# Nineteen small SBUF copies beside the last stores of a ReLU linear-attention kernel

## The chip, the cores and the metric

The kernel runs on one core of one Trainium2 chip. The metric is the device time of one execution in microseconds; the two runs of the kernel before took 126.61 and 126.70 us, with a median of 126.66 us. A profiled execution of the same kernel gives the trace that is read here. Its span, from the first to the last instruction, is 124.8 us.

## The reference

Q, K and V have the shape 8 x 12 x 512 x 64 in fp32, so there are 96 heads of 512 rows of 64 values.

```python
Q_feat = np.maximum(0, Q)
K_feat = np.maximum(0, K)
KV = np.einsum('bhkd,bhkv->bhdv', K_feat, V)
K_sum = np.sum(K_feat, axis=2)
numerator = np.einsum('bhqd,bhdv->bhqv', Q_feat, KV)
denominator = np.einsum('bhqd,bhd->bhq', Q_feat, K_sum)
return (numerator / (denominator[:, :, :, None] + 1e-10)).astype(np.float32)
```

Each input and the output is 12.6 MB in fp32. The trace counts 37.75 MB read from HBM and 12.58 MB written.

## The kernel before

**Tiling.** Eight heads make an octet, and there are twelve octets (`NO = 12`), numbered 0 to 11 in the code; the "tenth octet" is octet 9. K and V are loaded by groups of four heads, two groups to an octet. One octet of the output is one tile `o_sb` of 128 partitions by 2048 fp32, which is 1 MiB.

**Loads.** The first two K and V groups are loaded as fp32 by SP (SyncE) in four transfers at the very start (L115, L116), K and V of a group into the two halves of one tile. All other loads are issued by POOL (GpSimd), which converts fp32 to bf16 on the way: `load_kv` (L101 for a whole octet, L105 for single groups) and `load_q` (L109). They are traced in one loop ahead of all computation, so on POOL they are queued one behind the other: 12 of Q, 14 of K and 14 of V, 40 in all. The pool of K tiles and the pool of V tiles have six buffers each, the pool of Q tiles seven.

**Computation.** For each octet DVE and ACT prepare K and V (`prep`, L144 and L146; `prep_v`, L151 or L153), PE makes K'V (`mm_kv`, L158), ACT copies the result out (L168), PE transposes Q (L179), PE computes the transposed output (L209) and the denominators (L229), PE turns the output back (L247), and DVE multiplies by the reciprocal in `norm` (L253) into `o_sb`, in two halves.

**Stores.** `store(o, o_sb)` is called after the second `norm` of an octet and issues on SP. For octets 0 to 6 it issues first a copy of 128 bytes from the K tile of the octet five ahead into the tile `scratch` (L261): that copy waits for this load, and since SP takes its instructions in order, the store behind it waits too. Then it issues the 1 MiB store (L268). Octets 7 to 9 have only the store. The last octet is stored in two halves (L266), each behind its half of `norm`; octet 10 has one store. Nothing ever reads `scratch`. Over the whole program SP issues 24 transfers: 4 loads, 7 scratch copies, 11 whole stores and 2 half stores.

**Order.** The schedule is by hand (`tc.manual_schedule()`): each engine takes its instructions in the order in which the program names them, and the framework adds the semaphore waits. A DMA signals its landing by a semaphore. At the end of the program (L371) SP waits for every transfer that is still out.

Of the kernel before, what the change touches and what calls it, by code (L numbers as in the profile page):

```python
# [10 lines left out]
def kernel(  # L11
# [7 lines left out]
    nc = tc.nc  # L19
# [12 lines left out]
    NO = NG // 2  # L32
# [5 lines left out]
    fp32 = mybir.dt.float32  # L38
# [4 lines left out]
    def pool(name, bufs, **kw):  # L43
        return ctx.enter_context(tc.tile_pool(name=name, bufs=bufs, **kw))

    consts = pool("consts", 1)
# [18 lines left out]
    ident32 = consts.tile([P, P], fp32, name="ident32")  # L65
# [13 lines left out]
    mask = consts.tile([P, 2, 2], fp32, name="mask")  # L79
    scratch = consts.tile([1, D], bf16, name="scratch")  # L80

    mask_h = consts.tile([P, 8, 2], fp32, name="mask_h")

    qt_sb = [consts.tile([P, U, P], bf16, name=f"qt{i}") for i in range(NZ)]
# [174 lines left out]
    def store(o, o_sb):  # L259
        if o + DELAY < NO:  # L260
            nc.sync.dma_start(out=scratch, in_=k_sb[2 * (o + DELAY)][0:1, 0, :])  # L261
        Ov = Or[o].rearrange("p (r d) -> p r d", d=D)
        if o == NO - 1:
            for j in range(2):
                rs = slice(RQ // 2 * j, RQ // 2 * (j + 1))
                nc.sync.dma_start(out=Ov[:, rs], in_=o_sb[:, rs])  # L266
            return
        nc.sync.dma_start(out=Ov, in_=o_sb)  # L268

    def out_tile():  # L270
        return outp.tile([P, RQ, D], fp32, name="o_sb", tag="o_sb")
# [19 lines left out]
    def backs(o):  # L291
        o_sb = out_tile()
        for j in range(2):
            norm(o, j, back(o, j), o_sb)
        store(o, o_sb)
# [26 lines left out]
    o = NO - 2  # L322
# [15 lines left out]
    for i in range(2):  # L338
        relu_q(o + 1, i, transp(o + 1, i), nc.vector if i == 1 else None)
    norm(o, 1, ps, o_sb)  # L340
    store(o, o_sb)
    idle(5, o + 1)
    out_u(o + 1, 0)
# [32 lines left out]
```

## Time and profile before

| What | us |
|---|---|
| median of two runs | 126.66 |
| span of the profiled execution | 124.8 |
| PE busy | 84.2 |
| DVE busy | 81.2 |
| ACT busy | 78.8 |
| POOL busy | 26.1 |
| last `norm` (L253) starts / lasts | 117.1 / 1.2 |
| last half store issued / time to landing | 118.3 / 5.6 |

The times are those of one execution, counted from the first instruction. "SPq" is the queue of SP: its DMA instructions are listed with the time that the issue took, not the time of the transfer. "To landing" is the time from the start of the issue to the signal that the transfer is complete. Waits for the landing of a transfer stand as separate EVENT_SEMAPHORE instructions where the DMA instruction has another wait of its own. The DMA share is the mean busy share of the 16 DMA engines; records overlap a little, so it can exceed 1.

### The profile page before, as it was taken

How to read it: one execution, taken by the hardware profiler on the slowest of the kernel's cores; microseconds unless marked ns; L12 is line 12 of the kernel's file. 1: busy time of each engine (PE TensorE's matmuls, PEld its weight loads, DVE VectorE, ACT ScalarE, POOL GpSimd, SP SyncE). 2: the span in 40 equal slices, each digit the busy share in tenths (PEclk: the TensorE clock that was granted, in tenths of full speed). 3: DMA queues.
4: the chain of work that ended last, by engine and by line, in shares of the span. 5: the costliest groups of instructions: out<-in, count | busy, mean ns of one | idle time of the engine just before them, and what ended most of it. 6: DMA issues, size and time to landing. Idle time of an engine off the chain costs nothing.

```text
span 124.8 us, 2646 instructions
## 1 busy us (share of the span) xinstructions
PE 84.2 (67%) x1075; PEld 76.8 (62%) x1075; DVE 81.2 (65%) x176; ACT 78.8 (63%) x114; POOL 26.1 (21%) x46
## 2 busy tenths in 40 slices
PE   0041096988989898982994790999597397798400
PEld 0040095977978786871993790799495395788300
DVE  2615852979797988729727925965909909978700
ACT  0250639999898979955944973667759556747000
POOL 6922133222332223011121111124031000000000
PEclk9999999999999999999589998559999999999995
DMA  3999999999999999999999999999999999999993
GB/s 116 332 282 275 218 207 211 213 212 215 207 214 213 210 219 283 293 223 262 317 216 246 339 212 211 356 229 231 343 223 217 337 246 216 316 421 423 428 412 129
DMA packets 10492, 32.67 MB, mean 262 GB/s; under 512 B 1136, under 2 KB 1136, under 8 KB 9072
## 3 DMA queue, kind: packets, MB, share of 16 engines
q0 software_dynamic: 7808, 17.83, 74.5%
q1 hardware_dynamic: 2672, 14.68, 29.3%
q8 instruction: 8, 0.13, 0.4%
q14 instruction: 4, 0.03, 0.1%
HBM read 37.75 MB, written 12.58 MB: 403 GB/s over the span
## 4 chain that ended last, share of the span: by engine, by line
DVE 32%; DMA 30%; PE 22%; ACT 6%; issue 2%; SPq 1%; DVEq 1%; ACTq 0%
DMA v_sb<-in_V_dram 22%; DVE o_sb L253 15%; PE ps_kv L158 11%; DMA kv_first<-in_V_dram 8%; PE ps_bk L247 6%; DVE kf L144 5%; ACT kvd L168 3%; DVE vo L146 3%; PE ps_qt L179 3%; DVE vo L153 2%; DVE den L237 2%; DVE rec L241 2%; DVE own L232 2%; ACT qt L187 2%; ACT vo L151 1%
## 5 line engine op out<-in xcount | busy, mean ns | idle before, releaser
L158 PE MATMUL ps_kv<-vo,kf 128*128 128x132 bf16 x384 | 30.1, 240 | 18.9 <-ACT vo L151 8.0
L158 PEld LDWEIGHTS <-kf 128*128 128x128 bf16 x384 | 27.3, 107 | 20.5 <-DVE vo L146 10.8
L253 DVE TENSOR_TENSOR o_sb<-ps_bk,rec 128x1024 f32<-128x1024 f32 x24 | 28.3, 1219 | 11.3 <-PE ps_bk L247 11.3
L168 ACT CAST kvd<-ps_kv 64x260 bf16<-64x260 f32 (+1 forms) x54 | 18.7, 346 | 16.4 <-PE ps_kv L158 14.3
L211 ACT COPY ot_sb<-ps_ot 128x1024 f32<-128x1024 f32 x22 | 21.9, 1015 | 5.4 <-PE ps_ot L209 4.8
L247 PE MATMUL ps_bk<-ident,ot_sb 128*128 128x128 f32 x192 | 23.0, 273 | 0.0
L144 DVE TENSOR_SCALAR kf<-k_sb,mask 128x1024 bf16<-128x1024 bf16 x44 | 18.3, 458 | 6.6 <-DMA k_sb<-in_K_dram 6.6
L187 ACT ACTIVATE qt<-ps_qt 128x1024 bf16<-128x1024 bf16 x23 | 22.4, 1029 | 0.1
L247 PEld LDWEIGHTS ps_bk<-ident,ot_sb 128*128 128x128 f32 x192 | 20.8, 141 | 0.0
L209 PE MATMUL ps_ot<-qt,kvd 128*128 128x256 bf16 x88 | 13.5, 283 | 10.4 <-DVE o_sb L253 10.2
L209 PEld LDWEIGHTS <-kvd 128*128 128x128 bf16 x88 | 8.4, 100 | 13.1 <-issue 12.1
L179 PE MATMUL ps_qt<-ident,q_sb 128*128 128x128 bf16 x192 | 14.8, 238 | 0.0
L146 DVE TENSOR_SCALAR vo<-v_sb,mask 128x1024 bf16<-128x1024 bf16 x22 | 10.7, 484 | 5.6 <-DMA v_sb<-in_V_dram 5.6
L151 ACT ACTIVATE vo<-v_sb,mask 128x1024 bf16<-128x1024 bf16 x10 | 11.5, 1154 | 4.0 <-DMA v_sb<-in_V_dram 3.8
L179 PEld LDWEIGHTS <-q_sb 128*128 128x128 bf16 x192 | 13.5, 108 | 0.5 <-DMA q_sb<-in_Q_dram 0.2
L109 POOL DMA_DIRECT2D q_sb<-in_Q_dram x12 | 7.3, 612 | 20.4 <-DMA k_sb<-in_K_dram 10.2
L229 PEld LDWEIGHTS <-qt 128*128 128x128 bf16 x192 | 6.7, 96 | 4.8 <-ACT qt L187 3.4
L229 PE MATMUL ps_den<-kvd,qt 128*128 128x16 bf16 x192 | 7.5, 179 | 2.7 <-ACT qt L187 2.2
L101 POOL DMA_DIRECT2D v_sb<-in_V_dram x8 | 5.7, 718 | 11.5 <-DMA q_sb<-in_Q_dram 7.6
L101 POOL DMA_DIRECT2D k_sb<-in_K_dram x8 | 5.6, 704 | 9.3 <-DMA v_sb<-in_V_dram 5.5
L232 DVE SCALAR_TENSOR_TENSOR own<-ps_den,mask_h 128x256 f32<-128x256 f32 x12 | 5.0, 417 | 3.3 <-PE ps_den L229 3.3
L105 POOL DMA_DIRECT2D k_sb<-in_K_dram x6 | 3.4, 568 | 15.9 <-DMA k_sb<-in_K_dram 8.0
(29 smaller groups left out, 39.0 us busy)
## 6 DMA issues: line engine op xcount, KB each, us to landing
out_dram<-o_sb SPq DMA_DIRECT2D x11, 1024.0 KB, 8.8
q_sb<-in_Q_dram POOLq DMA_DIRECT2D x12, 512.0 KB, 20.1
k_sb<-in_K_dram POOLq DMA_DIRECT2D x8, 512.0 KB, 21.3
v_sb<-in_V_dram POOLq DMA_DIRECT2D x8, 512.0 KB, 21.1
k_sb<-in_K_dram POOLq DMA_DIRECT2D x6, 256.0 KB, 17.7
v_sb<-in_V_dram POOLq DMA_DIRECT2D x6, 256.0 KB, 17.0
kv_first<-in_K_dram SPq DMA_DIRECT2D x2, 512.0 KB, 5.7
kv_first<-in_V_dram SPq DMA_DIRECT2D x2, 512.0 KB, 7.2
```

What stands on the lines that cost most here:

```text
L144: nc.vector.tensor_scalar(kf[g][:, :, s, :], k_sb[g], scalar1=0.0, scalar2=mask[:, 0, s:s + 1], op0=Alu.max, op1=Alu.mult)
L146: nc.vector.tensor_scalar(vo[g % NB][:, :, 0, 2:D + 2], v_sb[g], scalar1=mask[:, 1, 0:1], scalar2=None, op0=Alu.mult)
L151: nc.scalar.activation(vo[g % NB][:, :, 1, 2:D + 2], v_sb[g], Act.Copy, scale=mask[:, 1, 1:2])
L158: nc.tensor.matmul(ps_kv[:, g % 2, 0:2 * (D + 2)].rearrange("p (t d) -> p t d", t=2), kf[g][:, r, :, :].rearrange("p s d -> p (s d)"), vo[ ...
L168: copy(kvd[o % NK][64 * c:64 * c + 64, 4 * gs.start + s:4 * gs.stop:2, c * D1:c * D1 + D1].rearrange("p (g t) d -> p g t d", t=2), ps_kv[6 ...
L179: nc.tensor.transpose(ps[:, u, :], q_sb[o][:, i * (U // 2) + u, :], ident)
L187: nc.scalar.activation(to, ps, Act.Relu)
L209: nc.tensor.matmul(ps[:, i], kvd[o % NK][:, h, 1:2 * D + 1], q[:, :, h, :], start=True, stop=True, skip_group_check=True)
L211: nc.scalar.copy(ot[o][:, :, 4 * j:4 * j + 4], ps.rearrange("p h u c -> p u h c"))
L229: nc.tensor.matmul(ps[:, u], qt_sb[o % NZ][:, u, :], kvd[o % NK][:, :, 0:2 * D1:2 * D1 - 1], start=True, stop=True, skip_group_check=True)
L247: nc.tensor.transpose(ps[:, 2 * v:2 * v + 2].rearrange("p c d -> p (c d)"), ot[o][:, 8 * j + v].rearrange("p h c -> p (h c)"), ident32)
L253: nc.vector.tensor_tensor(o_sb[:, rs], ps, rec[o][:, rs].unsqueeze(2).to_broadcast([P, 16, D]), op=Alu.mult)
```

## The change

A tile `marks` is added (16 partitions by 24 x 80 fp32, 7680 bytes in each partition). Behind the store of octet 9, SP issues fifteen copies from the identity matrix `ident32` (fp32, in SBUF) into rows of `marks`: the first has 15 partitions, the last has 1, and each has its own row size, 32 + 2k fp32 for k partitions (248 bytes for k = 15, 136 for k = 1). Each goes to a free-dimension range of `marks` that no other copy writes. Four more, of 3, 5, 2 and 1 partitions with rows of 64 + 2k fp32, are issued by GpSimd; in the program they come at the same place, but since GpSimd has only the loads in its queue ahead of them, they stand directly behind its last load. Nobody reads `marks`; the output and its computation are as before.

```diff
@@ -79,6 +79,7 @@
     scratch = consts.tile([1, D], bf16, name="scratch")
 
+    marks = consts.tile([16, 24, 80], fp32, name="marks")
     mask_h = consts.tile([P, 8, 2], fp32, name="mask_h")
@@ -266,6 +267,11 @@
             return
         nc.sync.dma_start(out=Ov, in_=o_sb)
+        if o == NO - 3:
+            for k in range(15, 0, -1):
+                nc.sync.dma_start(out=marks[0:k, k, 0:32 + 2 * k], in_=ident32[0:k, 0:32 + 2 * k])
+            for k in (3, 5, 2, 1):
+                nc.gpsimd.dma_start(out=marks[0:k, 16 + k, 0:64 + 2 * k], in_=ident32[0:k, 0:64 + 2 * k])
 
     def out_tile():
```

## The prediction

> **What bounds the kernel now.** I read the engine table first (PE 67%, DVE 65%, ACT 63%: no engine is full), then the chain of waits, then the stages of the tail, then SP's queue. The chain ends with the last `norm`; what follows it is only the store of its result. The table of stages shows what the tail is (us, then busy us and instruction counts of PE, PEld, DVE, ACT and POOL, then granted clock, DMA share, GB/s):
>
> ```profile
> 105.00:110.00 5.00, 4.14 (x52) 3.83 (x49) 4.93 (x13) 2.98 (x6) 0.00 (x0) 1.00 1.07 316
> 110.00:115.00 5.00, 4.47 (x72) 3.91 (x70) 4.14 (x8) 3.14 (x5) 0.00 (x0) 1.00 1.01 421
> 115.00:120.00 5.00, 1.79 (x17) 1.56 (x15) 2.36 (x2) 0.44 (x1) 0.00 (x0) 1.00 1.00 419
> 120.00:124.80 4.80, 0.00 (x0) 0.00 (x0) 0.00 (x0) 0.00 (x0) 0.00 (x0) 0.64 0.57 230
> ```
>
> The DMA engines are full from 105 us to 121 us: the stores of octets 6 to 11 drain one behind the other. At 419 GB/s a store of 1.049 MB takes 2.5 us. SP's queue (start, issue time) shows why they come together:
>
> ```profile
> 102.78 0.50 SPq L261 DMA_DIRECT2D scratch<-k_sb  x1
> 103.37 10.70 SPq L268 DMA_DIRECT2D out_dram<-o_sb  x5
> 117.21 1.46 SPq L266 DMA_DIRECT2D out_dram<-o_sb  x2
> ```
>
> The scratch copy of octet 6 held the queue until 102.8; four stores (octets 6 to 9) then go out within 2.2 us. The tenth octet's store, and the one after it, one by one:
>
> ```profile
> 105.19 0.33 SPq L268 DMA_DIRECT2D out_dram<-o_sb  x1
> ...
> 113.74 0.33 SPq L268 DMA_DIRECT2D out_dram<-o_sb  x1
> ```
>
> Between them SP stands idle for 8.2 us, and that is where the fifteen copies go. The first of the two lands late:
>
> ```profile
> L268 SPq DMA_DIRECT2D out_dram<-o_sb x1: 333/333/333, 105.2 to 105.2; - x1
> L268 SPq EVENT_SEMAPHORE  x1: 17/17/17, 105.6 to 105.6; - x1
> ...
> DMA to landing us min/median/max: 13.9/13.9/13.9
> ```
>
> 13.9 us after 105.2 is 119.1 us: that is when octet 9's store is complete. The EVENT_SEMAPHORE at 105.6 belongs to the next store (octet 10): a second wait beside that for `norm`. It is the key of this prediction. What it waits for is seen best on POOL at the start:
>
> ```profile
> 1.24 0.65 POOL L109 DMA_DIRECT2D q_sb<-in_Q_dram  x1 [0.79 <-POOLq L360]
> ...
> 6.47 0.71 POOL L101 DMA_DIRECT2D k_sb<-in_K_dram  x1
> 9.43 0.72 POOL L101 DMA_DIRECT2D v_sb<-in_V_dram  x1 [2.25 <-DMA q_sb<-in_Q_dram]
> 13.41 0.56 POOL L109 DMA_DIRECT2D q_sb<-in_Q_dram  x1 [3.27 <-DMA k_sb<-in_K_dram]
> ```
>
> The load at 9.43 is POOL's ninth, and only the third of V, whose pool has six buffers; so it waits for no buffer, yet it waits for the landing of POOL's first load (Q). The tenth waits for the second (K). An engine thus has eight landing semaphores in rotation, and its ninth transfer waits until the first has landed. SP does the same:
>
> ```profile
> L268 SPq EVENT_SEMAPHORE  x7: 17/17/17, 64.3 to 105.6; - x7
> L266 SPq EVENT_SEMAPHORE  x1: 17/17/17, 117.6 to 117.6; - x1
> ```
>
> On whole stores the extra wait begins at 64.3, the third octet's store, SP's tenth transfer. It is missing just where the transfer eight places earlier is a scratch copy that SP had already waited for (octets 7 and 9, first half of octet 11). Today all these waits are for transfers long landed (17 ns each): octet 10's store waits for octet 4's.
>
> **The change, part by part.** Call the copies c1 to c15. In SP's order there now stand: store 6, 7, 8, 9, c1 ... c15, store 10, store 11 in halves. Counting eight back:
> - c1 to c4 wait for store 4, scratch 5, store 5 and scratch 6, issued by 102.8; scratch 6 needs 4.8 us and lands at 107.6. They go out between 105.6 and 108, in SP's idle time: nothing.
> - c5, c6 and c7 wait for stores 6, 7 and 8. These landed 8.1, 10.2 and 12.2 us after 103.37, 103.95 and 104.47, so at 111.5, 114.2 and 116.7. From here SP is held, store 10 (ready at 113.7) behind it.
> - c8 waits for store 9: 119.1 us. The copies queued behind that store cannot shift its landing.
> - c9 to c15 wait for c1 to c7, which sit in the queue behind store 9 and carry 19 KB together. I take it that they land within a few tenths of 119.1, so these waits cost nothing; only the issues count.
>
> So from 119.1 on, SP has to issue eight copies, c8 to c15, before store 10. The trace has no copy of this shape. The nearest row is the scratch copy, also small and SBUF to SBUF: 0.50 us, with 0.05 to 0.09 to the next, so 0.55. The lower bound is the cheapest issue on SP, 0.33 + 0.05 = 0.38. Above, nothing in the trace bounds an issue with fewer than 16 rows; as an estimate I take twice the scratch copy, 1.0. A cost below nothing is excluded, since each is an instruction on an in-order queue. At 0.55 the eight take 4.4 us (3.0 to 8.0), and store 10 is issued at 123.5 rather than 113.7. It also waits for c8 to land; even with the 4.8 us of a scratch copy that is 123.9, 0.4 later, and the queues are then empty, so I leave that out. Stores 11 wait for c9 and c10, issued 0.55 and 1.1 after c8: nothing more.
>
> By 123.5 the DMA engines have been idle for over 4 us, and 2 MiB are still to go. An issue into empty queues is seen once: the first K load (L115), 0.52 MB, landed 3.4 us after its issue at 0.74. At 419 GB/s its data take 1.25, so 2.15 are latency. Store 10 and the two halves need 2.15 + 2 x 2.5 = 7.1 us; their last landing is at 130.6. Before, it was 118.34 + 5.6 = 123.9. From there to the end of the span was 0.9 us, which stays. **Sum: 130.6 - 123.9 = +6.7 us**, a span of 131.5. The median stood 1.84 us above the span; 131.5 + 1.84 = 133.3.
>
> The last `norm` ends at 118.3 as before and is now 6 us ahead of its store; DVE, PE and ACT have nothing to wait for, since no tile is needed again.
>
> **The four on GpSimd.** POOL issues its last load at 94.4 and does nothing after. Transfer 41 to 44 wait for 33 to 36, of 40 loads; the last load lands 16.2 us after 94.4, at 110.6, and these are all earlier. POOL pays 4 x 0.53 us (its row for L109) in idle time; the eleven rows queue behind the last load in POOL's own queue. Should they disturb DVE or the last loads by their whole 2.1 us, the norms would end at 120.4, still 3 us ahead of the store. So nothing; if the store were not late, up to 2.1 us. The tile `marks` moves other tiles' addresses, at no cost that a row shows.
>
> **The rivals.**
> 1. *Issue time only* (not slower): the copies take no part in the rotation, or are not issued at all. Then fifteen issues of 0.55 are 8.25 us, from 105.6 to 113.8, beside 113.7 for store 10: 0.1 us late, with store 9 still draining until 119. As an issue takes at most 2.15 us to become data, store 10 could go as late as 116.9 without a gap, which is 0.75 us a copy; from there it decides. Time 126.7. Against it: every one of SP's transfers obeys the rotation, the scratch copies too, and these are listed seven times though nobody reads them. The Trainium skill, page "DMA: Bandwidth & Descriptors", section "Issuing engines are not separate DMA queues", calls the sequencer's time to initiate a DMA usually small relative to the DMA itself; by that rule this rival would hold. Chance 0.07.
> 2. *Dearer issues*: the mechanism as forecast, 0.65 to 1.0 us a copy: 0.8 to 3.6 us more, 134.1 to 136.9. For it: no row with such a shape. Chance 0.12.
> 3. *Each copy waits for the one before*, as they write one tile: fourteen more landings of 2.15 us behind c1's, 30 us instead of 4.4: about 159. Against it: the first K and V loads write the halves of one tile, and their issues at 0.74 and 1.19 follow without a wait. [...] Chance 0.03.
> 4. *Faster*: the profile shows nothing that a later store would free. Chance 0.03 for what I don't see.
>
> **How the numbers follow.** The forecast has 0.75. Its own range is 131.9 (0.38 a copy) to 134.1 (0.65). The range reaches below to 131.2, if the latency is 0.7 less than the load showed, and above to 137.0 for rival 2; it leaves out rivals 1, 3 and 4, 0.13, and the forecast's own rest. About 2%, 2.5 us, is what a measurement of this kernel can tell from no change. Slower: 0.75 + 0.12 + 0.03 = 0.90; same 0.07; faster 0.03.
>
> **What would show it.** Right: SP's queue shows four copies at 105.6 to 108, then single ones at 111.5, 114.2, 116.7 and 119.1, then a burst of seven and store 10 at about 123.5; waits of SP for the landings of `out_dram` appear ahead of the copies; GB/s falls to nearly nothing between 119 and 124, then shows 2 MiB at over 400; PE, DVE and ACT end as before. Wrong: store 10 at about 113.8 and no gap (rival 1), copies 2 us apart (rival 3), or a burst of 8 us (rival 2). If c9 to c15 wait for landings of their own, c1 to c7 landed later than I take them to.

## The result and the profile after

The changed kernel takes 134.13 us (median of two runs, 133.90 and 134.37) against 126.66 us: 7.5 us more, a ratio of 1.0588 with a 95% interval of 1.0562 to 1.0613. The profiled execution has a span of 132.6 us against 124.8, so 7.8 us more. Lines of the code have moved: the whole stores are now L269, the half stores L267, the SP copies L272, the GpSimd copies L274, `norm` L254, the end of the program L377.

SP's queue (start, issue time):

```profile
103.28 0.50 SPq L262 DMA_DIRECT2D scratch<-k_sb  x1
103.88 2.05 SPq L269 DMA_DIRECT2D out_dram<-o_sb  x4
105.98 19.06 SPq L272 DMA_DIRECT2D marks<-ident  x15
125.14 0.34 SPq L269 DMA_DIRECT2D out_dram<-o_sb  x1
125.58 1.33 SPq L267 DMA_DIRECT2D out_dram<-o_sb  x2
```

The fifteen copies occupy SP's queue for 19 us, and the store of octet 10 is issued at 125.1 instead of 113.7. Of the 19 us only 10.7 are issue time. How the copies lie in time is seen from three cuts of the same line (issue time in ns: least, median, most; first and last start in us), one ahead of 110, one between 111 and 118, one after 119:

```profile
L272 SPq DMA_DIRECT2D marks<-ident x4: 734/799/942, 106.0 to 108.7; - x4
...
L272 SPq DMA_DIRECT2D marks<-ident x3: 722/722/758, 112.1 to 117.0; - x3
...
L272 SPq DMA_DIRECT2D marks<-ident x8: 578/672/717, 119.5 to 124.5; - x8
```

Four at once, three one at a time, then a burst of eight. What separates them is in SP's list of waits (us in total, times, longest):

```profile
SPq L272 <- DMA out_dram<-o_sb: 7.8, 4, 2.7
```

Four copies waited for landings of whole stores, up to 2.7 us each, although they read the identity matrix and write a tile of their own. The trace also records the number of the semaphore that each transfer of SP waits for and signals when it lands. The eighth copy waits for and signals number 115, which octet 9's store signals; the first eight copies go through eight different numbers, the next seven through the first seven of these again in the same order, and octet 10's store waits for 115 once more, now the eighth copy's. In the stages the DMA engines run dry (columns as in the table of stages of before; the last three are granted clock, DMA share and GB/s):

```profile
110.00:115.00 5.00, 4.41 (x56) 4.18 (x55) 2.93 (x5) 1.80 (x4) 0.00 (x0) 0.93 1.03 427
115.00:120.00 5.00, 3.67 (x51) 3.27 (x47) 3.93 (x6) 2.03 (x2) 0.00 (x0) 1.00 0.59 241
120.00:125.00 5.00, 0.00 (x0) 0.00 (x0) 0.30 (x1) 0.00 (x0) 0.00 (x0) 0.59 0.02 3
125.00:130.00 5.00, 0.00 (x0) 0.00 (x0) 0.00 (x0) 0.00 (x0) 0.00 (x0) 0.50 0.82 333
```

From 120 to 125 they move 3 GB/s, with 2 MiB of output still to be stored; PE and ACT are done and DVE has 0.3 us of work left. The moment at which SP has seen the last landing can be read from its DRAIN instructions at the end, in before and after:

```profile
L371 SPq DRAIN  x3: 7/7/7, 124.0 to 124.3; - x3
```

```profile
L377 SPq DRAIN  x3: 7/7/7, 131.7 to 132.1; - x3
```

The last landing moved by 7.7 us, of the 7.8 by which the spans differ.

### The profile page after: what moved, and what is told of

It reads as the page before. It is cut to its first block, busy times and chain, and to the rows that moved or that the text cites. A ratio compares the mean times of both kernels' runs of the same rounds, so it can differ in the third digit from the quotient of the medians.

```text
span 132.6 us, 2666 instructions
## 1 busy us (share of the span) xinstructions
PE 86.5 (65%) x1075; PEld 78.9 (60%) x1075; DVE 81.4 (61%) x176; ACT 79.0 (60%) x114; POOL 27.7 (21%) x50
## 4 chain that ended last, share of the span: by engine, by line
DMA 54%; PE 15%; DVE 14%; ACT 3%; issue 1%; SPq 1%; DVEq 1%; ACTq 0%
DMA k_sb<-in_K_dram 34%; DMA q_sb<-in_Q_dram 12%; DMA kv_first<-in_V_dram 8%; DVE o_sb L254 7%; PE ps_kv L159 6%; PE ps_bk L248 5%; PE ps_qt L180 2%; ACT kvd L169 2%; DVE kf L145 2%; ACT qt L188 1%; PE ps_ot L210 1%; DVE vo L147 1%; DVEq L377 1%; DVE den L238 1%; SPq L116 1%
## 5 line engine op out<-in xcount | busy, mean ns | idle before, releaser
L159 PE MATMUL ps_kv<-vo,kf 128*128 128x132 bf16 x384 | 29.6, 238 | 19.6 <-ACT vo L152 7.9
L254 DVE TENSOR_TENSOR o_sb<-ps_bk,rec 128x1024 f32<-128x1024 f32 x24 | 28.3, 1218 | 13.8 <-PE ps_bk L248 13.8
L248 PE MATMUL ps_bk<-ident,ot_sb 128*128 128x128 f32 x192 | 23.9, 279 | 0.0
L248 PEld LDWEIGHTS ps_bk<-ident,ot_sb 128*128 128x128 f32 x192 | 21.8, 146 | 0.0
L210 PE MATMUL ps_ot<-qt,kvd 128*128 128x256 bf16 x88 | 14.4, 294 | 9.3 <-DVE o_sb L254 9.3
L180 PE MATMUL ps_qt<-ident,q_sb 128*128 128x128 bf16 x192 | 16.1, 250 | 0.1
L180 PEld LDWEIGHTS <-q_sb 128*128 128x128 bf16 x192 | 14.8, 115 | 0.8 <-DMA q_sb<-in_Q_dram 0.3
L110 POOL DMA_DIRECT2D q_sb<-in_Q_dram x12 | 6.8, 570 | 20.1 <-DMA k_sb<-in_K_dram 13.9
```

The source lines that it names most:

```text
L159: nc.tensor.matmul(ps_kv[:, g % 2, 0:2 * (D + 2)].rearrange("p (t d) -> p t d", t=2), kf[g][:, r, :, :].rearrange("p s d -> p (s d)"), vo[ ...
L180: nc.tensor.transpose(ps[:, u, :], q_sb[o][:, i * (U // 2) + u, :], ident)
L210: nc.tensor.matmul(ps[:, i], kvd[o % NK][:, h, 1:2 * D + 1], q[:, :, h, :], start=True, stop=True, skip_group_check=True)
L248: nc.tensor.transpose(ps[:, 2 * v:2 * v + 2].rearrange("p c d -> p (c d)"), ot[o][:, 8 * j + v].rearrange("p h c -> p (h c)"), ident32)
L254: nc.vector.tensor_tensor(o_sb[:, rs], ps, rec[o][:, rs].unsqueeze(2).to_broadcast([P, 16, D]), op=Alu.mult)
```

## The experiments

Two theories stood against each other at first. By R, the rotation of eight landing semaphores holds SP until octet 9's store has landed, and the time lost is what the DMA engines then stand idle. By its rivals the loss comes from the number of copies, from SP's issue time or from the GpSimd copies. The edits shown are against the changed kernel, and all ratios against runs of the kernel before on the same chip.

### One part alone

```diff
-            for k in range(15, 0, -1):
-                nc.sync.dma_start(out=marks[0:k, k, 0:32 + 2 * k], in_=ident32[0:k, 0:32 + 2 * k])
```

> Only the four GpSimd copies and the tile marks are kept; SP has no copies. Theory R (the rotation of eight landing semaphores holds SP's queue): the four cost nothing, 126.7 us, within 0.5 us of the kernel before; store of octet 10 issued at about 113.7, last norm ends near 118.3. Rival P (the GpSimd copies take part in the loss, through DVE or the last loads): up to 2.1 us later norms and 127 to 129 us.

Measured: 127.03 us, ratio 1.0022 (1.0001 to 1.0043). The reverse edit leaves out the two lines of GpSimd:

> The fifteen SP copies alone, none by GpSimd. Theory R: the whole loss is here, 133.9 to 134.4 us. Rival P (the GpSimd copies add something once the others are there): 0.5 us or more below the whole change, 133.5 or less.

Measured: 134.12 us, ratio 1.0567 (1.055 to 1.0585). The whole loss is in the SP copies. In the run with the GpSimd copies alone the last two halves of `norm` ran like this:

```profile
117.63 2.36 DVE L254 TENSOR_TENSOR o_sb<-ps_bk,rec 128x1024 f32<-128x1024 f32 x2 [1.00 <-PE ps_bk L248]
```

They end at 120.0, 1.7 us later than in before, and the span is only 0.4 us longer (125.2): the DMA engines are full up to 121 (a share of 0.98 to 1.03 in each two microseconds from 113 on), so `norm` has slack there. The expectation that `norm` would end near 118.3 was wrong; the likely cause, a stretch with a low granted clock on PE, stands in the section on what was not expected.

### How many copies it takes

```diff
-            for k in range(15, 0, -1):
+            for k in range(15, 9, -1):
```

> Six SP copies (15 to 10 partitions) instead of fifteen. Theory R: the store of octet 10 waits for the landing of octet 8's store (116.7 to 117.1), the first half of octet 11 for octet 9's (119.1 to 119.5), with data still queued all the time: no gap in the DMA engines, 126.7 us, at most 127.3. Rival I (only SP's issue time counts, whatever the place): also 126.7. Rival L (loss in proportion to the copies): 0.4 x 7.5 = 3.0 us more, 129.7.

Measured: 127.22 us, ratio 1.003 (1.0019 to 1.0041). SP's queue:

```profile
106.92 8.48 SPq L272 DMA_DIRECT2D marks<-ident  x6
117.01 0.34 SPq L269 DMA_DIRECT2D out_dram<-o_sb  x1
119.45 0.84 SPq L267 DMA_DIRECT2D out_dram<-o_sb  x2
```

Octet 10's store now waits for a landing itself (from SP's list of waits):

```profile
SPq L269 <- DMA out_dram<-o_sb: 1.6, 1, 1.6
```

One copy more (`range(15, 8, -1)`):

> Seven SP copies (15 to 9 partitions), one more than in six. Theory R: now the store of octet 10 waits for octet 9's landing, at 119.1 to 119.5; the queues run empty for about a microsecond; store 10 and the halves need 6.5 us from that issue: last landing 125.6 to 126.0 against 123.9, so 128.4 to 128.8 us; the step from six to seven is 1.5 to 2.1 us although it is one small copy. Rival I: seven issues of 0.8 fit into the 8.2 us, 126.7. Rival L: 130.2, a step of 0.5.

Measured: 129.47 us (four runs, 128.33 to 129.60), ratio 1.0194 (1.0147 to 1.0242). SP's queue, and the wait of octet 10's store from SP's list of waits:

```profile
107.00 10.78 SPq L272 DMA_DIRECT2D marks<-ident  x7
119.53 0.34 SPq L269 DMA_DIRECT2D out_dram<-o_sb  x1
119.98 1.32 SPq L267 DMA_DIRECT2D out_dram<-o_sb  x2
...
SPq L269 <- DMA out_dram<-o_sb: 1.7, 1, 1.7
```

The stages from 117 to 121 us, first with six copies, then with seven:

```profile
117.00:119.00 2.00, 1.13 (x11) 0.90 (x9) 1.70 (x2) 0.00 (x0) 0.00 (x0) 1.00 0.97 389
119.00:121.00 2.00, 0.00 (x0) 0.00 (x0) 0.66 (x1) 0.00 (x0) 0.00 (x0) 0.79 1.00 400
```

```profile
117.00:119.00 2.00, 1.22 (x12) 0.99 (x9) 1.61 (x2) 0.00 (x0) 0.00 (x0) 1.00 0.56 218
119.00:121.00 2.00, 0.00 (x0) 0.00 (x0) 0.74 (x1) 0.00 (x0) 0.00 (x0) 0.91 0.33 136
```

With six, the store of octet 10 goes out 3.3 us later than in before and the DMA engines stay full; with seven it goes out 2.5 us later still, when the store it waits for (octet 9's) has landed, and they run dry. The seventh copy, an issue of 0.72 us, costs 2.2 us of time. Neither issue time (which would still fit into SP's idle time) nor a loss in proportion to the number explains a step at that place. The size was 0.7 to 1.1 us above what R expected. In the trace, which is that of the slowest of the four runs, SP sees the last landing 7.5 us after the issue of octet 10's store, against 6.5 reckoned. The DMA engines move 401 GB/s from 120.4 to 125.4, but then only 49 GB/s for another microsecond, where the changed kernel has no such end; why a small part of the data lags is not settled.

### The price of an issue

All SP copies get 16 partitions; their row sizes stay as they are.

```diff
-                nc.sync.dma_start(out=marks[0:k, k, 0:32 + 2 * k], in_=ident32[0:k, 0:32 + 2 * k])
+                nc.sync.dma_start(out=marks[0:16, k, 0:32 + 2 * k], in_=ident32[0:16, 0:32 + 2 * k])
```

> All fifteen SP copies have 16 partitions (row sizes as before). Theory R holds SP until octet 9's store lands (119.1 to 119.5) in any case; eight issues follow. Price theory S (an issue with 16 rows is as cheap as the scratch copy, 0.55 with the gap; fewer rows, spread unevenly, are dear): 4.4 us, store 10 issued at 123.7, 132.6 us, faster than the fifteen of uneven size. Price theory G (the price grows with the rows, from 0.58 at one partition to 0.94 at fifteen): 0.95 to 1.0 each, 7.6 to 8 us, store 10 at 127.2, 136 to 136.5 us.

Measured: 133.75 us, ratio 1.0551 (1.053 to 1.0573). The copies after 119 us, and the store behind them:

```profile
L272 SPq DMA_DIRECT2D marks<-ident x8: 507/587/589, 119.4 to 123.8; - x8
...
DMA to landing us min/median/max: 1.6/1.7/2.3
```

```profile
124.44 0.53 SPq L269 DMA_DIRECT2D out_dram<-o_sb  x1
```

Price theory G falls: sixteen rows do not cost more than fifteen but less, 0.51 to 0.59 us an issue. Price theory S has the direction and not the size: with the gaps the eight take 5.0 us (119.41 to 124.44), 0.63 each, between the 0.55 of S and the 0.71 of the uneven copies. The interval of this run overlaps with those of the changed kernel (1.0588) and of the SP copies alone (1.0567), so the gain in time is not shown; the price is read from the traces. SP is held at the same places as with the uneven copies, the eighth copy starting at 119.41, although more rows are queued; so it is the number of transfers that counts, and not the number of rows.

### The same copies in other places

Two behind octet 4's store, seven behind octet 5's, six behind octet 9's:

```diff
-        if o == NO - 3:
-            for k in range(15, 0, -1):
+        for at, ks in ((4, (15, 14)), (5, range(13, 6, -1)), (NO - 3, range(6, 0, -1))):
+            for k in ks if o == at else ():
```

> All nineteen copies, in other places of SP's queue: two behind octet 4's store, seven behind octet 5's, six behind octet 9's. Counted eight back, each copy and each store now waits for a transfer that has landed by then, or (stores 10 and 11) for one whose landing comes while data are still queued. Theory R: no gap, as with six copies, 126.7 to 127.3 us. Rival N (nineteen small transfers cost about 7 us wherever they stand, by their number): 133 to 134.

Measured: 127.08 us, ratio 1.0025 (1.0013 to 1.0038). SP's queue:

```profile
83.87 1.81 SPq L272 DMA_DIRECT2D marks<-ident  x2
...
94.00 5.43 SPq L272 DMA_DIRECT2D marks<-ident  x7
...
105.75 9.26 SPq L272 DMA_DIRECT2D marks<-ident  x6
116.90 0.34 SPq L269 DMA_DIRECT2D out_dram<-o_sb  x1
119.36 0.84 SPq L267 DMA_DIRECT2D out_dram<-o_sb  x2
```

All nineteen copies are there, and 0.3 us is left of the 7.5. The loss does not belong to the copies but to what stood eight transfers ahead of them. The opposite case puts all fifteen behind octet 5's store:

```diff
-        if o == NO - 3:
+        if o == 5:
             for k in range(15, 0, -1):
                 nc.sync.dma_start(out=marks[0:k, k, 0:32 + 2 * k], in_=ident32[0:k, 0:32 + 2 * k])
+        if o == NO - 3:
             for k in (3, 5, 2, 1):
```

> The same fifteen copies behind octet 5's store (issued at 93.7) instead of octet 9's. The eighth waits for octet 5's landing (103.0), eight issues of 0.7 follow, so octet 6's store goes out at 109.2 instead of 103.9: a hold of 5.3 us. Theory G (a hold costs only what it leaves the DMA engines idle): the last loads fill them until about 108, a gap of 1 to 2 us, 127.7 to 128.8 us. Rival H (each us of hold on a store is a us of time): 5.3 more, 132.

Measured: 129.59 us, ratio 1.0225 (1.0198 to 1.0252). The stages around the hold, in before and in this run:

```profile
107.00:109.00 2.00, 2.00 (x28) 2.00 (x26) 1.93 (x7) 1.45 (x5) 0.00 (x0) 1.00 1.05 365
109.00:111.00 2.00, 2.00 (x30) 1.76 (x28) 1.61 (x4) 0.40 (x2) 0.00 (x0) 1.00 1.00 412
```

```profile
107.00:109.00 2.00, 1.15 (x18) 1.24 (x19) 1.93 (x7) 0.92 (x1) 0.00 (x0) 1.00 0.70 130
109.00:111.00 2.00, 2.00 (x24) 1.95 (x23) 2.00 (x5) 1.06 (x4) 0.00 (x0) 1.00 0.52 193
```

The octet 6 store goes out at 109.2, as reckoned, 5.8 us later than in before, and the time grows by 2.8 us: half of the hold, so rival H falls. Theory G of this run (a hold costs only what it leaves the DMA engines idle) has the mechanism and a size too small (1 to 2 us). Counted in bytes it comes closer: over these four microseconds 2 x (365 - 130) + 2 x (412 - 193) = 908 KB fewer are moved than in before, which is 2.2 us at 419 GB/s.

### What is left over

The runs without a gap stood 0.2 to 0.3% above the kernel before. Two more kernels looked for the cause: the six SP copies without those of GpSimd, and the kernel before with the line of the tile `marks` and no copy.

> Six SP copies behind octet 9's store as in the run with six, and none by GpSimd. The runs with the four GpSimd copies but no gap in the tail stood 0.2 to 0.3 per cent (0.2 to 0.4 us) above the kernel before. If the GpSimd copies are the cause, this one is at 1.000 (within 0.15 per cent); if the SP copies or the tile are, it is at 1.002 to 1.003 again.

> The tile marks is allocated and no copy is made. If the tile's place in SBUF (other tiles move by 7680 bytes) costs the 0.2 to 0.3 per cent, it is here too, 1.002 to 1.003; if the copies do, this is at 1.000 within 0.15 per cent.

Measured: six SP copies alone 1.0014 (0.9999 to 1.0028), the tile alone 0.9993 (0.9977 to 1.0009). The tile's place in SBUF costs nothing that can be seen. The first result lies at the upper edge of the lower expectation, and its interval reaches into the other, so which copies make up the 0.3 us stays open.

## Why the prediction was right

It gave 133.3 us and a range of 131.2 to 137.0; measured are 134.13, at the upper end of the forecast's own range (131.9 to 134.1) and just inside that of the dearer issues. Direction and mechanism were right; two terms were mis-sized, and that they partly cancel is luck. Point by point:

- **The rotation.** The forecast had c1 to c4 free, c5, c6 and c7 at 111.5, 114.2 and 116.7, and c8 at 119.1. The trace has four at 106.0 to 108.7, then 112.1, 114.6, 117.0 and 119.5, and just four waits for stores. The held ones lie 0.3 to 0.6 us later; the scratch copy of octet 6 had gone out at 103.28 instead of 102.78. The step from six to seven copies, and the spread copies, show that it is the place in the rotation that decides, and the semaphore numbers in the trace are those of a rotation of eight.
- **c9 to c15 wait for nothing that counts.** Right: the eight follow each other from 119.5 without a gap.
- **The price of an issue.** This is the main term that was mis-sized. Taken were 0.55 us from the scratch copy; the eight took 5.66 us (119.48 to 125.14), 0.71 each instead of 4.4 in all. That is 1.3 us too little, and within the rival of dearer issues (0.65 to 1.0), whose mechanism is the same. The scratch copy, which the trace records as 16 pieces of 8 bytes, was the wrong neighbour for two reasons that the 16-row run separates: back to back, even copies of sixteen rows take 0.63 with their gaps, and uneven row numbers add the rest.
- **Two MiB into empty queues.** Reckoned 7.1 us; SP sees the last landing at 131.7, 6.5 to 6.6 after the issue at 125.14. The reckoning was 0.5 too much, and the surplus sits in the 2.15 us of latency taken from the first load. In the trace of before no data move until 1.75, 1.0 us after that load's issue, and then only 164 GB/s for 0.75 us; so a part of the 2.15 was a slow start and not latency. In the changed kernel the stores' data begin 0.8 us after the issue and run at 405 GB/s from 126 to 131.
- **The sum in the trace.** 0.4 for the later start, 1.3 for the issues, less 0.5 for the transfer, makes 1.2 more than the 6.7 us of the forecast; the spans differ by 7.8, so 1.1 more.
- **The GpSimd copies at nothing.** Right within 0.3 us. They waited as foretold for transfers 33 to 36. POOL's queue shows the first two; the others, at 101.43 and 103.55, waited for a load of Q and one of K:

```profile
96.11 0.52 POOL L274 DMA_DIRECT2D marks<-ident  x1 [0.45 <-DMA k_sb<-in_K_dram]
97.31 0.50 POOL L274 DMA_DIRECT2D marks<-ident  x1 [0.68 <-DMA v_sb<-in_V_dram]
```

- **`norm` ends as before.** Wrong by 2.0 us (120.3 instead of 118.3), without effect, since the half stores go out at 125.6 and later.
- **The rivals.** Issue time alone falls by the step from six to seven. Its turning point, 116.9 reckoned for the first gap, is bracketed and no more: a store at 117.0 costs at most 0.4 us, one at 119.5 costs 2.6 over the kernel before. Landing by landing falls too: from 119.5 the copies are 0.7 us apart, while in the 16-row run the landing of such a copy takes 1.6 to 2.3 us. The Trainium skill's sentence on issue time ("DMA: Bandwidth & Descriptors", section "Issuing engines are not separate DMA queues": the sequencer's time to initiate a DMA is usually small relative to the DMA itself) does not hold for copies as small as these, with 0.51 to 0.59 us an issue beside those landings in the 16-row run.

## What to carry to other kernels

Before a transfer is put into an in-order queue, count back through that queue by the number of landing semaphores (eight here) and ask when the transfer found there lands; then do the same for the transfers behind the new one, whose partners have moved too. A small transfer behind a backlog of large ones waits for the backlog (in the 16-row run the first three copies land 12.8 to 13.6 us after their issue, the last eight 1.6 to 2.3), and whatever is queued behind it goes out into empty engines. The delay itself is not the loss: it counts only from the point at which the data already queued run out.

## What had not been expected of the hardware

- The issue time of a copy on SP goes with its number of rows and is not monotonic: 0.94 us with fifteen partitions, 0.84 with fourteen, 0.72 to 0.76 with nine to thirteen, 0.66 with eight, 0.72 with seven, 0.58 with one (recorded as two pieces of 68 bytes), but 0.51 to 0.59 with sixteen. The place matters little: the same copies in the spread run and behind octet 5's store differ by at most 0.07 us. Nor does the row size, which changes from copy to copy in the 16-row run too. What in the number of rows makes the price is not shown.
- PE's granted clock fell to about half in the tail of eight of the eleven traces, at places that changed from run to run: 0.63 and then 0.52 from 101 to 105 us with the GpSimd copies alone, 0.57 to 0.58 between 107 and 111 us in the changed kernel. In before, in the spread run and with the tile alone it was 1.00 from 99 to 113. The last `norm` ends 1.0 to 2.0 us later than in before in the eight, and at most 0.1 us later in the other two; of the 2.0 in the changed kernel, 0.4 stood already at 103, ahead of the stretch. The time shows little of it: the runs without a gap are at most 0.3% above the kernel before, since the DMA engines were the bound.
